# Rebuilding a mixer's decay weights without GpSimd, and scheduling small matmuls of one tiling as one operation

## The chip, the cores and the metric

One core of one Trainium2 chip. The metric is the device time in microseconds of one execution; lower is better. The kernel's engines are named as in the profile: PE (TensorE matmuls), PEld (TensorE weight loads), DVE (VectorE), ACT (ScalarE), POOL (GpSimd) and SP (SyncE, which issues the DMAs).

## What is computed

The network has two blocks over 512 tokens of width 1024 and a context of 256 tokens, all in fp32. The first block has two layers. Layer 0 mixes tokens with a gated delta rule (8 heads of width 128, both directions, called GDN here), layer 1 with a state space model (32 heads of width 64 in 8 groups of 4, both directions, called SSD here). Each layer ends in a mixture of 16 experts (MoE). A second block follows, which the change doesn't touch.

For the change two pieces of it matter. In SSD each head's output inside its stretch of 128 tokens is a weighted sum whose weights are

```python
acs = jnp.cumsum(dt_i * A, axis=1)
seg = jnp.where(tril, acs[:, :, None] - acs[:, None, :], -jnp.inf)
wts = jnp.einsum('btgn,bsgn->btsg', c_i, b_i)[..., None] * jnp.exp(seg) * dt_i[:, None]
```

The kernel makes the weights of both directions in one 128 x 512 tile W per head (four stretches of 128 x 128): exp of the smaller of the two directions' differences, times a factor Dm (dt of the forward direction on one side of the diagonal, dt of the backward one on the other), times the product of C and B, which the four heads of a group share. In GDN a triangular system of each stretch of 128 tokens is inverted: blocks of 32 by elimination, then blocks of 64 and 128 by products of blocks. Besides, six vectors per layer modulate the activations (the "ada" product, a 1024 x 6144 matrix for each layer times two vectors).

## The kernel before, in words

Every instruction is recorded first (`Rec.add`, line 126) with what it reads and writes, and a planner orders a whole stage at once (`Rec.flush`, line 217, and `Rec.schedule`, line 280). `Rec.cost` (line 164) gives each operation a duration, `LATENCY` (line 210) a delay between engines, and the planner takes, again and again, the operation that can start first, with a rank for ties that comes from the order in the program and the length of the chain behind it. Its result is one fixed order per engine; at run time each engine works through its own list in order. A stage may try several ranks and keep the best by its own count: GDN one, SSD three. An operation of PE writing to a PSUM tile is ordered behind earlier ones on the same 32 partitions of that tile. All instructions are issued from one line, 277, so the profile tells groups apart by tile names alone.

The stages, each one `flush`: the first norm and the first ada round (0 to 42 us), GDN (to about 800), the MoE's routing and gathering (to 850) and experts (to 1490), SSD's groups (to about 2080), SSD's output product, the second MoE, and block 2 from about 2760.

**The ada product** (`Mod.round`, line 937). One round is 8 k-steps; each k-step has four matmuls whose stationary operand is 32 columns wide (`self.sc`), each 128 x 512 and each writing another 32 partitions of one PSUM tile, so that they sit in four different column strips of the array. Each of the four is an operation of its own for the planner, and waits for its own 256 KB of weights. Round 0 is planned by itself, four rounds lie in GDN (as side work of heads 0, 6 and 7), one in the gathering of the first MoE. An fp32 matmul appears as two records in the trace.

**GDN** (`gdn`, line 550). Per head: four projections (tile px), each a product of split operands (a weight w is split into wh, its rounding, on ACT, and wl, the rest, on DVE or POOL, and three matmuls take the place of one); the squared norms of q and k (tile ssq, lines 689 to 695: two matmuls of 32 columns for q, then two for k); matrices L, GE and `at`; the elimination of 32 x 32 blocks on POOL (tiles x and D, 30 steps of two instructions); the inverse's products; and a scan of six steps. The inverse's products (lines 790 to 816) are, for blocks of 32 and then of 64, pB = L times U, and pU = T times B; for 64 the transpose pT comes first, as `pe.transpose` where d = 0 and as a matmul with the identity where d = 1. The loops run over the diagonal position (`cut`, 4 or 2 values, each a part of the array of its own) outside and over the six stretches of tokens inside. All outputs of one product lie in one PSUM tile.

**SSD** (`ssd`, line 1417). A preamble makes dt and the running sums cs, and writes their rows to DRAM. Then 8 groups of 4 heads; per head (lines 1495 to 1511):

```python
nc.sync.dma_start(x.rearrange("p t i -> p (t i)"), dbc(rscr[32 * d + h], 128))
g_.tensor_tensor(x, x, cs[:, :, 32 * d + h:32 * d + h + 1].to_broadcast([128, 4, 128]), op=OP.subtract)
...
v.tensor_tensor(W, R[0], R[1], op=OP.min)
s.activation(W, W, AF.Exp)
...
g_.tensor_tensor(Dm, K.m_le[:, None, :].to_broadcast([128, 4, 128]), dt[:, 0:4, h:h + 1].to_broadcast([128, 4, 128]), op=OP.mult)
...
v.tensor_tensor(W, W, Dm, op=OP.mult)
```

that is, per head, three POOL instructions of 128 x 512 (two on R, one on Dm), on DVE one minimum, four 128 x 128 pieces of Dm and one product, and one exp on ACT. After it come the group's four projections of x, B and C (px, pcx) and two of z (pz), whose low parts wl are made on DVE, for C and z on POOL; transposes (ptr), states (st), the product cb of C and B, its copy cbs on ACT, one DVE product of each W with cbs (line 1591), the heads' outputs py (16 matmuls of 64 columns in two PSUM tiles), the part from the states (pi, er), and the sums y and ssq, some of them on POOL. W has 4 buffers, R 4, Dm 1, cbs 2. The ring for weights holds 18 pieces.

Of the kernel before, what the change touches and what calls it, by code (L numbers as in the profile page):

```python
# [11 lines left out]
F32 = mybir.dt.float32  # L12
# [40 lines left out]
class Rec:  # L53
# [71 lines left out]

    def add(self, engine, method, a, k):
        reads, writes = [], []
# [8 lines left out]
        i = len(self.ops)  # L136
# [16 lines left out]
        if engine == "tensor":  # L153
            r = ww[0]
            key = r[0] + "#pe"
            q = (key, r[1] // 32 * 32, -(-r[2] // 32) * 32, 0, 1)
            lst = self.access.setdefault(key, [])
            preds.update(j for j, _, z in lst if q[1] < z[2] and z[1] < q[2])
# [3 lines left out]
        self.ops.append(dict(e=engine, m=method, a=a, k=k, preds=preds, names=names, cost=self.cost(engine, method, reads, writes, a, k), psum=any(self.tiles.get(r[0], (0, 0, 0))[2] for r in rr + ww)))  # L162
# [54 lines left out]
    def flush(self, trials=((0.0, 30.0),)):  # L217
# [166 lines left out]
KT = 8  # L384
# [165 lines left out]
def gdn(K, H, apply, w, ba_w, conv_w, a_log, dt_b, norm_g, scr, bscr, tscr, rscr, side, xc, w_out, gate, route):  # L550
# [111 lines left out]
    for h in range(NH):  # L662
# [27 lines left out]
        for j, a in enumerate((q, k_)):  # L690
            sq = per.tile([128, TT], F32, name="sq", tag="th", bufs=2)
            s.activation(sq, a, AF.Square, scale=0.5)
            for f in range(2):
                c = 32 * (2 * j + f)
                pe.matmul(pq[c:c + 32, :], K.ones[:, 0:32], sq[:, f * 384:(f + 1) * 384], start=True, stop=True)
# [94 lines left out]
        for m in (32, 64):  # L790
# [15 lines left out]
            for d, ra, ca in cut:  # L806
                for t in range(6):
                    pe.matmul(p[ra, t, :], L[ca, t, ra], Ud[ca, 1 - d, t, :] if m == 32 else U[ca, d, t, ca], start=True, stop=True, skip_group_check=True)
# [3 lines left out]
            for d, ra, ca in cut:  # L812
                for t in range(6):
                    pe.matmul(p[ra, t, :], Tr[d][ra, t, :], B[ra, t, :], start=True, stop=True, skip_group_check=True)
# [112 lines left out]
class Mod:  # L927
# [9 lines left out]
    def round(self, r):  # L937
# [479 lines left out]
def ssd(K, H, apply, w, wz, w_dt, conv_w, conv_b, a_log, dt_b, d_skip, norm_g, w_out, gate, keep, scr, rscr, side, route):  # L1417
# [46 lines left out]
    K.softplus(dt, a, tmp, sh, "W", 4)  # L1464
# [8 lines left out]
    for dst, ms in ((cs, (mid[:, 0, :], mid[:, 1, :])), (ea, (K.m_le, K.m_ge)), (we, (K.m_gt, K.m_lt)), (et, (K.ones, K.ones))):  # L1473
# [5 lines left out]
        s.activation(dst, p, AF.Copy if dst is cs else AF.Exp)  # L1479
    for j, x in enumerate((cs, ea)):  # L1480
# [4 lines left out]
        s.activation(rows, p.rearrange("p t i -> p (t i)"), AF.Copy)  # L1485
# [5 lines left out]
    for g in range(8):  # L1491
# [96 lines left out]
        cbs = grp.tile([128, 4, 128], F32, name="cbs", bufs=2)  # L1588
        s.activation(cbs, pcb, AF.Copy)
        for W in Ws:  # L1590
            v.tensor_tensor(W, W, cbs, op=OP.mult)
        py = [K.ps([128, 512], "py") for _ in range(2)]
        for i in range(2):
            for t in range(4):
                for r in range(2):
                    h = 2 * i + r
                    pe.matmul(py[i][64 * r:64 * r + 64, t * 128:(t + 1) * 128], xt[:, t, h * 64:(h + 1) * 64], Ws[h][:, t, :], start=(t == 0), stop=(t == 3))
# [887 lines left out]
```

## Time and profile before

| | us |
|---|---|
| median of 3 runs | 3717.8 (3711.24 to 3721.67) |
| the profiled execution | 3719.51 |
| its span, first to last instruction | 3717.7 |
| PE busy | 3442.1 (93%) |
| DVE busy | 1914.3 (51%) |
| ACT busy | 1105.9 (30%) |
| POOL busy | 662.7 (18%) |

The profile is one execution. "Busy" is the time in which at least one instruction of the engine runs; PE's records overlap, and their ends are modelled. The view by stretches gives, for each stretch of time, the busy time and instruction count of each engine, the granted TensorE clock (1.00 is 2.4 GHz, the lower level is 1.2) and the DMA engines' share. A view of one tile gives the shortest, median and longest duration of each kind of instruction on it.

### The profile page before, as it was taken

Reading aid. Unit: us, or ns where it says so; the run is one execution under the profiler, and the core shown is the slowest. Engines: PE = TensorE matmul, PEld = TensorE weight load, DVE = VectorE, ACT = ScalarE, POOL = GpSimd, SP = SyncE. Lnnn points to the kernel's source line nnn. Section 1 sums busy time; section 2 is a strip of 40 time slices with the busy share of each in tenths; the row PEclk is TensorE's granted clock in tenths of the full one; section 3 lists DMA queues with packets and bytes.
Section 4 is the critical chain, followed back from the end, with each engine's and each line's share of the span. In section 5 each row is a group of like instructions: output and inputs, shape, how many; then the busy total and the mean of one; then the engine's idle time right before and its main releaser. Section 6 shows DMA issues by size and latency. Waiting matters only on the chain. (4 is left out here: it accounts for less than half of the span.)

```text
span 3717.7 us, 55087 instructions
## 1 busy us (share of the span) xinstructions
PE 3442.1 (93%) x21457; PEld 2310.9 (62%) x21457; DVE 1914.3 (51%) x4006; ACT 1105.9 (30%) x2270; POOL 662.7 (18%) x849
## 2 busy tenths in 40 slices
PE   7999998899999999889999779988879999999999
PEld 4777775656444454667777664332247657878887
DVE  4657754453223222798888551371254574445552
ACT  3355443423111111433333322020032343333331
POOL 0546544301000000154444011020001000000000
PEclk9989999899999999999999889999999999999999
DMA  5422137354888887343333349899972302333332
GB/s 193 151 54 66 54 85 244 123 187 162 348 313 322 333 321 298 115 119 102 115 106 101 129 181 365 357 369 410 420 214 77 120 1 91 94 105 85 97 87 87
DMA packets 251649, 669.18 MB, mean 180 GB/s; under 512 B 72156, under 2 KB 85612, under 8 KB 202236
## 3 DMA queue, kind: packets, MB, share of 16 engines
q1 hardware_dynamic: 251388, 665.66, 50.7%
q8 instruction: 169, 2.77, 0.3%
q14 instruction: 92, 0.75, 0.1%
HBM read 644.26 MB, written 21.30 MB: 179 GB/s over the span
## 5 line engine op out<-in xcount | busy, mean ns | idle before, releaser
L277 DVE TENSOR_TENSOR wl<-w,wh 128x512 fp32r<-128x512 f32 (+3 forms) x452 | 320.9, 713 | 443.2 <-PE fu L277 67.6
L277 ACT ACTIVATE wh<-w 128x512 fp32r<-128x512 f32 (+3 forms) x500 | 307.0, 621 | 620.8 <-PE fu L277 120.6
L277 PE MATMUL eg<-we,xs 128*32 128x512 f32 (+1 forms) x1536 | 374.2, 597 | 9.5 <-DMA we<-moe_w 8.3
L277 PE MATMUL eu<-we,xs 128*32 128x512 f32 (+1 forms) x1536 | 324.4, 595 | 7.6 <-DMA we<-moe_w 7.6
L277 PE MATMUL ey<-we,hTs 128*32 128x512 f32 (+1 forms) x1536 | 295.9, 599 | 12.0 <-ACT hTs L277 9.0
L277 PE MATMUL px<-H,wl 128*128 128x512 f32 (+1 forms) x768 | 271.3, 372 | 6.4 <-DVE wl L277 6.4
L277 PE MATMUL px<-H,wh 128*128 128x512 f32 (+1 forms) x768 | 272.9, 376 | 2.8 <-ACT wh L277 1.6
L277 PE MATMUL px<-H1l,wh 128*128 128x512 f32 (+1 forms) x768 | 272.8, 369 | 0.0
L277 PE MATMUL ec<-we,xs 128*32 128x512 f32 x1024 | 237.5, 594 | 0.0
L277 DVE TENSOR_TENSOR yl<-ey,yh 64x512 fp32r<-64x512 f32 x64 | 44.1, 689 | 330.7 <-ACT yh L277 330.1
L277 POOL TENSOR_TENSOR wl<-w,wh 128x512 fp32r<-128x512 f32 x48 | 64.4, 1345 | 738.0 <-DVE H1l L277 651.5
L277 PEld LDWEIGHTS eg<-we,xs 128*32 128x32 f32 (+1 forms) x1536 | 98.7, 119 | 139.8 <-issue 94.6
L277 DVE SCALAR_TENSOR_TENSOR eth<-eth,eg 128x512 f32<-128x512 f32 x32 | 22.0, 688 | 312.9 <-ACT eth L277 312.9
L277 PEld LDWEIGHTS eu<-we,xs 128*32 128x32 f32 (+1 forms) x1536 | 94.8, 119 | 139.7 <-issue 97.2
L277 PEld LDWEIGHTS ey<-we,hTs 128*32 128x32 f32 (+1 forms) x1536 | 98.6, 120 | 120.9 <-issue 60.9
L277 PEld LDWEIGHTS px<-H,wh 128*128 128x128 f32 x768 | 146.3, 194 | 30.3 <-issue 6.4
L277 PEld LDWEIGHTS px<-H,wl 128*128 128x128 f32 x768 | 145.2, 194 | 28.9 <-DVE wl L277 8.5
L277 PEld LDWEIGHTS px<-H1l,wh 128*128 128x128 f32 x768 | 145.2, 194 | 23.3 <-issue 4.6
L277 ACT ACTIVATE eth<-eg 128x512 f32<-128x512 f32 x32 | 19.1, 596 | 463.2 <-PE eg L277 434.4
L277 PE MATMUL eyc<-we,hcTs 128*32 128x256 f32 x1024 | 143.4, 379 | 0.0
L277 POOL TENSOR_TENSOR x<-D 48x30 f32<-48x30 f32 (+14 forms) x240 | 127.1, 530 | 90.8 <-DVE D L277 73.9
L277 POOL TENSOR_TENSOR D<-D,x 48x30 f32<-48x30 f32 (+14 forms) x240 | 133.6, 557 | 17.9
(1041 smaller groups left out, 7816.1 us busy)
## 6 DMA issues: line engine op xcount, KB each, us to landing
we<-moe_w SPq DMA_DIRECT2D x384, 1024.0 KB, 7.2
w<-ada_w SPq DMA_DIRECT2D x192, 256.0 KB, 4.9
w<-w_gu SPq DMA_DIRECT2D x88, 256.0 KB, 3.0
w<-gdn_w SPq DMA_DIRECT2D x64, 256.0 KB, 3.2
w<-ssd_w SPq DMA_DIRECT2D x64, 256.0 KB, 4.0
R<-ssd_rows SPq DMA_DIRECT2D x64, 256.0 KB, 4.7
w<-w_mix SPq DMA_DIRECT2D x48, 256.0 KB, 2.7
w<-w_dn SPq DMA_DIRECT2D x40, 256.0 KB, 2.6
```

What stands on the lines that cost most here:

```text
L277: getattr(getattr(self.nc, o["e"]), o["m"])(*o["a"], **o["k"])
```

## The change

`Rec.together()` is a new context: the PE operations recorded inside it become one operation of the planner, with their dependencies united and their costs added, and are issued back to back. It is put around: the four ada matmuls of a k-step; the four squared-norm matmuls of a GDN head (both squares are now made first, in two tiles); pT, pB and pU of the inverse, each, with the loops turned round (six stretches outside, diagonal positions inside); and each PSUM tile of py (8 matmuls). In pT the transposes become matmuls with the identity for both values of d.

SSD's decays leave POOL. The rows of the forward direction are loaded into W itself (6 buffers), those of the backward one into R (3 buffers). Per stretch of 128 tokens ACT adds the column of -cs to W (`Identity` with a bias), and DVE takes, in one instruction, R plus its column and the minimum. After exp, W is not touched until cb is there. From cb DVE makes two masked copies per group, cb0 and cb1, straight from PSUM; per head and stretch ACT scales cb0 by dt and DVE adds cb1 times the other dt (tile Dm, in R's buffers); one product of W with Dm ends it.

```diff
+    @contextmanager
+    def together(self):
+        assert self.run is None
+        self.run = []
+        yield
+        self.run = None
...
+        if i < len(self.ops):
+            o = self.ops[i]
+            o["preds"] |= preds
+            o["names"] |= names
+            o["cost"] += cost
+            o["more"].append((method, a, k))
+            return
...
-            getattr(getattr(self.nc, o["e"]), o["m"])(*o["a"], **o["k"])
+            for m, a, k in [(o["m"], o["a"], o["k"])] + o.get("more", []):
+                getattr(getattr(self.nc, o["e"]), m)(*a, **k)
...
+        sqs = []
+        for a in (q, k_):
+            sqs.append(per.tile([128, TT], F32, name="sq", tag="th", bufs=2))
+            s.activation(sqs[-1], a, AF.Square, scale=0.5)
+        with nc.together():
+            for c in range(4):
+                j, f = divmod(c, 2)
+                pe.matmul(pq[32 * c:32 * c + 32, :], K.ones[:, 0:32], sqs[j][:, f * 384:(f + 1) * 384], start=True, stop=True)
...
-                for d, ra, ca in cut:
+                with nc.together():
                     for t in range(6):
-                        if d:
+                        for d, ra, ca in cut:
                             pe.matmul(p[ra, t, :], U[ra, d, t, ra], K.ident[ra, ra], start=True, stop=True, skip_group_check=True)
-                        else:
-                            pe.transpose(p[ra, t, :], U[ra, d, t, ra], K.ident[ra, ra])
...
-            for d, ra, ca in cut:
+            with nc.together():
                 for t in range(6):
-                    pe.matmul(p[ra, t, :], Tr[d][ra, t, :], B[ra, t, :], start=True, stop=True, skip_group_check=True)
+                    for d, ra, ca in cut:
+                        pe.matmul(p[ra, t, :], Tr[d][ra, t, :], B[ra, t, :], start=True, stop=True, skip_group_check=True)
...
-            for c in range(4):
-                nc.tensor.matmul(p[32 * c:32 * c + 32, :], self.sc[:, k, :], wt[:, c, :], start=(k == 0), stop=(k == KT - 1))
+            with nc.together():
+                for c in range(4):
+                    nc.tensor.matmul(p[32 * c:32 * c + 32, :], self.sc[:, k, :], wt[:, c, :], start=(k == 0), stop=(k == KT - 1))
...
-                x = tmp.tile([128, 4, 128], F32, name="R", bufs=4)
+                x = tmp.tile([128, 4, 128], F32, name="WR"[d], bufs=6 - 3 * d)
                 nc.sync.dma_start(x.rearrange("p t i -> p (t i)"), dbc(rscr[32 * d + h], 128))
-                g_.tensor_tensor(x, x, cs[:, :, 32 * d + h:32 * d + h + 1].to_broadcast([128, 4, 128]), op=OP.subtract)
                 R.append(x)
-            W = tmp.tile([128, 4, 128], F32, name="W", bufs=4)
-            v.tensor_tensor(W, R[0], R[1], op=OP.min)
+            W = R[0]
+            for t in range(4):
+                s.activation(W[:, t, :], W[:, t, :], AF.Identity, bias=cs[:, t, h:h + 1])
+                v.scalar_tensor_tensor(W[:, t, :], R[1][:, t, :], cs[:, t, 32 + h:33 + h], W[:, t, :], op0=OP.add, op1=OP.min)
             s.activation(W, W, AF.Exp)
-            Dm = tmp.tile([128, 4, 128], F32, name="Dm", bufs=1)
-            g_.tensor_tensor(Dm, K.m_le[:, None, :].to_broadcast([128, 4, 128]), dt[:, 0:4, h:h + 1].to_broadcast([128, 4, 128]), op=OP.mult)
-            for t in range(4):
-                v.scalar_tensor_tensor(Dm[:, t, :], K.m_ge, dt[:, t, 32 + h:33 + h], Dm[:, t, :], op0=OP.mult, op1=OP.add)
-            v.tensor_tensor(W, W, Dm, op=OP.mult)
             Ws.append(W)
...
-        cbs = grp.tile([128, 4, 128], F32, name="cbs", bufs=2)
-        s.activation(cbs, pcb, AF.Copy)
-        for W in Ws:
-            v.tensor_tensor(W, W, cbs, op=OP.mult)
+        cbs = [grp.tile([128, 4, 128], F32, name=f"cb{d}", bufs=1) for d in range(2)]
+        for cb_, m in zip(cbs, (K.m_le, K.m_ge)):
+            v.tensor_tensor(cb_, pcb, m[:, None, :].to_broadcast([128, 4, 128]), op=OP.mult)
+        for r, W in enumerate(Ws):
+            h = 4 * g + r
+            Dm = tmp.tile([128, 4, 128], F32, name="Dm", tag="R", bufs=3)
+            for t in range(4):
+                s.activation(Dm[:, t, :], cbs[0][:, t, :], AF.Copy, scale=dt[:, t, h:h + 1])
+                v.scalar_tensor_tensor(Dm[:, t, :], cbs[1][:, t, :], dt[:, t, 32 + h:33 + h], Dm[:, t, :], op0=OP.mult, op1=OP.add)
+            v.tensor_tensor(W, W, Dm, op=OP.mult)
```

## Rows read from the trace of the kernel before

**Rows 1.** Stretches: length, busy PE, PEld, DVE, ACT, POOL (count); clock, DMA share, GB/s

```profile
78.00:581.00 503.00, 470.94 (x3449) 374.42 (x3448) 320.41 (x870) 231.70 (x544) 256.14 (x426) 0.94 0.32 92
...
760.00:850.00 90.00, 79.14 (x504) 49.57 (x503) 54.40 (x118) 20.04 (x50) 4.33 (x6) 0.92 0.48 173
...
1581.00:2046.00 465.00, 427.86 (x2290) 352.06 (x2289) 409.34 (x610) 157.21 (x278) 227.06 (x178) 0.95 0.36 108
2046.00:2080.00 34.00, 20.15 (x125) 15.28 (x123) 25.42 (x45) 10.67 (x20) 7.49 (x7) 0.80 0.18 60
```

**Rows 2.** PE's waits, 1581 to 2046: us in total, times, longest

```profile
PE pz L277 <- POOL wl L277: 19.2, 5, 4.5
PE st L277 <- DVE xw L277: 6.8, 8, 1.7
```

**Rows 3.** DVE's groups by line and shape, 1581 to 2046

```profile
L277 DVE SCALAR_TENSOR_TENSOR Dm<-cst,dt,Dm 128x128 f32<-128x128 f32 x124 | 100.0, 861 | 2.6 <-POOL Dm L277 2.6
L277 DVE TENSOR_TENSOR W<-R 128x512 f32<-128x512 f32 x32 | 34.8, 1102 | 0.0
L277 DVE TENSOR_TENSOR W<-W,Dm 128x512 f32<-128x512 f32 x32 | 30.4, 949 | 0.9
L277 DVE TENSOR_TENSOR W<-W,cbs 128x512 f32<-128x512 f32 x28 | 21.3, 759 | 1.3 <-ACT cbs L277 1.3
```

**Rows 4.** Tiles Dm and R: shortest/median/longest ns, first and last start

```profile
L277 DVE SCALAR_TENSOR_TENSOR Dm<-cst,dt,Dm x128: 334/1130/1451, 1578.7 to 2032.6; 128x128 f32<-128x128 f32 x128
...
L277 DVE TENSOR_TENSOR W<-R x32: 672/1030/1789, 1589.7 to 2023.1; 128x512 f32<-128x512 f32 x32
```

**Rows 5.** POOL's groups, 1581 to 2046

```profile
L277 POOL TENSOR_TENSOR R<-R,cs 128x512 f32<-128x512 f32 x64 | 79.9, 1264 | 31.6 <-DMA R<-ssd_rows 15.1 <-ACT xt L277 8.5 <-DVE W L277 4.7
L277 POOL TENSOR_TENSOR wl<-w,wh 128x512 fp32r<-128x512 f32 x42 | 55.2, 1318 | 68.4 <-DMA w<-ssd_w 20.1 <-PE pz L277 19.0 <-DVE wl L277 9.7
...
L277 POOL TENSOR_TENSOR Dm<-cst,dt 128x512 f32<-128x512 f32 x31 | 34.9, 1126 | 28.9 <-DVE W L277 27.4 <-DMA ssd_scratch<-y 1.5
```

**Rows 6.** ACT's scaled 128x128 copy in GDN (tile vb)

```profile
L277 ACT ACTIVATE vb<-vT,cols x96: 386/399/407, 99.9 to 735.6; 128x128 f32<-128x128 f32 x96
```

**Rows 7.** ACT's longest wait in SSD's groups, and the DMA of R

```profile
ACT W L277 <- DVE W L277: 130.8, 27, 10.2
...
R<-ssd_rows SPq DMA_DIRECT2D x64, 256.0 KB, 4.7
```

**Rows 8.** PE in order of time: one ada matmul alone, then four together

```profile
126.02 1.05 PE L277 MATMUL ada<-w,sc 128*32 128x512 f32 x2
...
112.65 1.06 PE L277 MATMUL ada<-w,sc 128*32 128x512 f32 x8
```

**Rows 9.** Tile ada alone, by stretches: length, busy PE, PEld, ACT; clock, DMA

```profile
78.00:552.00 474.00, 18.50 (x64) 2.75 (x64) 0.60 (x1) 0.94 0.29 82
552.00:760.00 208.00, 49.83 (x192) 8.63 (x192) 1.79 (x3) 0.95 0.57 177
760.00:850.00 90.00, 20.53 (x64) 3.26 (x64) 0.60 (x1) 0.92 0.48 173
```

**Rows 10.** Tile ssq alone, one stretch: length, busy PE, PEld, DVE, ACT, POOL

```profile
78.00:552.00 474.00, 13.23 (x56) 2.19 (x56) 0.00 (x0) 3.43 (x7) 0.00 (x0) 0.94 0.29 82
```

**Rows 11.** PE in order of time: pU of two heads, the start of pB for 64

```profile
205.48 0.86 PE L277 MATMUL pU<-B,Td 32*32 32x32 f32 x48
...
353.14 1.21 PE L277 MATMUL pU<-B,Td 32*32 32x32 f32 x48 [0.60 <-ACT B L277]
...
355.41 0.39 PE L277 MATMUL pB<-U,L 64*64 64x64 f32 x5
...
357.59 0.39 PE L277 MATMUL px<-H1l,wh 128*128 128x256 f32 x1
358.72 1.31 PE L277 MATMUL pU<-B,Tr 64*64 64x64 f32 x24
```

**Rows 12.** POOL in order of time: the elimination of GDN's head 6 starts

```profile
581.38 0.24 POOL L277 TENSOR_TENSOR x<-D 48x30 f32<-48x30 f32 x1 [18.14 <-DVE D L277]
```

More of the change, by code (lines that the diff above doesn't have):

```diff
@@ L3 @@
 import math
-from contextlib import ExitStack
+from contextlib import ExitStack, contextmanager
 import numpy as np
@@ L124, in region, with record @@
         return name, p0, last // row + 1, 0, row * size
-    def add(self, engine, method, a, k):
+    @contextmanager
[3 more added lines that the diff above has]
+        yield
+        self.run = None
+    def add(self, engine, method, a, k):
+        if self.run is None or engine != "tensor":
+            return self.record(len(self.ops), engine, method, a, k)
+        if not self.run:
+            self.run.append(len(self.ops))
+            self.record(self.run[0], engine, method, a, k)
+            self.ops[-1]["more"] = []
+        else:
+            self.record(self.run[0], engine, method, a, k)
+    def record(self, i, engine, method, a, k):
         reads, writes = [], []
@@ L157, in add @@
             lst = self.access.setdefault(key, [])
-            preds.update(j for j, _, z in lst if q[1] < z[2] and z[1] < q[2])
+            preds.update(j for j, _, z in lst if j != i and q[1] < z[2] and z[1] < q[2])
             lst[:] = [t for t in lst if not (q[1] <= t[2][1] and t[2][2] <= q[2])]
@@ L161, in add @@
         names = {r[0] for r in rr + ww}
-        self.ops.append(dict(e=engine, m=method, a=a, k=k, preds=preds, names=names, cost=self.cost(engine, method, reads, writes, a, k), psum=any(self.tiles.get(r[0], (0, 0, 0))[2] for r in rr + ww)))
+        cost = self.cost(engine, method, reads, writes, a, k)
+        if i < len(self.ops):
[5 more added lines that the diff above has]
+            return
+        self.ops.append(dict(e=engine, m=method, a=a, k=k, preds=preds, names=names, cost=cost, psum=any(self.tiles.get(r[0], (0, 0, 0))[2] for r in rr + ww)))
     def cost(self, engine, method, reads, writes, a, k):
@@ L689, in gdn @@
         pq = K.ps([128, 384], "ssq")
[L690 to L695, printed above, removed]
+        sqs = []
[6 more added lines that the diff above has]
+                pe.matmul(pq[32 * c:32 * c + 32, :], K.ones[:, 0:32], sqs[j][:, f * 384:(f + 1) * 384], start=True, stop=True)
         sq = K.nm.tile([128, 512], F32, name="ssq_", tag="nm", bufs=3)
@@ L805, in gdn @@
             p = K.ps([128, 6, m], "pB")
-            for d, ra, ca in cut:
+            with nc.together():
                 for t in range(6):
-                    pe.matmul(p[ra, t, :], L[ca, t, ra], Ud[ca, 1 - d, t, :] if m == 32 else U[ca, d, t, ca], start=True, stop=True, skip_group_check=True)
+                    for d, ra, ca in cut:
+                        pe.matmul(p[ra, t, :], L[ca, t, ra], Ud[ca, 1 - d, t, :] if m == 32 else U[ca, d, t, ca], start=True, stop=True, skip_group_check=True)
             B = tmp.tile([128, 6, m], F32, name=f"B{m}")
@@ L943, in round @@
             wt = K.wtile(self.w[r, k], [128, 4, 512])
-            for c in range(4):
-                nc.tensor.matmul(p[32 * c:32 * c + 32, :], self.sc[:, k, :], wt[:, c, :], start=(k == 0), stop=(k == KT - 1))
+            with nc.together():
+                for c in range(4):
+                    nc.tensor.matmul(p[32 * c:32 * c + 32, :], self.sc[:, k, :], wt[:, c, :], start=(k == 0), stop=(k == KT - 1))
         row = K.nm.tile([128, 512], F32, name="adarow", tag="nm", bufs=3)
@@ L1463, in ssd @@
     v.tensor_tensor(a, p, al[:, 1:2, :].to_broadcast(sh), op=OP.add)
-    K.softplus(dt, a, tmp, sh, "W", 4)
+    K.softplus(dt, a, tmp, sh, "W", 6)
     v.scalar_tensor_tensor(a, dt, -1.0, al[:, 0:1, :].to_broadcast(sh), op0=OP.mult, op1=OP.mult)
@@ L1478, in ssd @@
             pe.matmul(p[:, :, c], ms[d], a[:, 0:n, c], start=True, stop=True)
-        s.activation(dst, p, AF.Copy if dst is cs else AF.Exp)
+        if dst is cs:
+            s.activation(dst, p, AF.Copy, scale=-1.0)
+        else:
+            s.activation(dst, p, AF.Exp)
     for j, x in enumerate((cs, ea)):
@@ L1484, in ssd @@
         rows = K.nm.tile([64, 512], F32, name="rows", tag="nm", bufs=3)
-        s.activation(rows, p.rearrange("p t i -> p (t i)"), AF.Copy)
+        s.activation(rows, p.rearrange("p t i -> p (t i)"), AF.Copy, scale=1.0 if j else -1.0)
         nc.sync.dma_start(rscr[64 * j:64 * j + 64], rows)
@@ L1587, in ssd @@
             pe.matmul(pcb[:, t, :], BT[:, t * 128:(t + 1) * 128], CT[:, t * 128:(t + 1) * 128], start=True, stop=True)
-        cbs = grp.tile([128, 4, 128], F32, name="cbs", bufs=2)
-        s.activation(cbs, pcb, AF.Copy)
-        for W in Ws:
-            v.tensor_tensor(W, W, cbs, op=OP.mult)
+        cbs = [grp.tile([128, 4, 128], F32, name=f"cb{d}", bufs=1) for d in range(2)]
[8 more added lines that the diff above has]
+            v.tensor_tensor(W, W, Dm, op=OP.mult)
         py = [K.ps([128, 512], "py") for _ in range(2)]
         for i in range(2):
[L1594 to L1597, printed above, removed]
+            with nc.together():
+                for t in range(4):
+                    for r in range(2):
+                        h = 2 * i + r
+                        pe.matmul(py[i][64 * r:64 * r + 64, t * 128:(t + 1) * 128], xt[:, t, h * 64:(h + 1) * 64], Ws[h][:, t, :], start=(t == 0), stop=(t == 3))
         for i in range(2):
```

3 lines of the change are left out of this document (1 added, 2 removed).

## The prediction

> **What bounds the kernel now.** I read the page first: PE is busy 93% of the span, so a time can only fall where PE waits or where its own work shrinks. Then the view by stretches for the three stages that the change touches [rows 1]. In GDN (78 to 581 us) PE is busy 470.9 of 503 us: PE is the bound, and its own work counts. In SSD's groups (1581 to 2046) PE is busy 427.9 of 465 us, but DVE is busy 409.3, 88%, and the granted clock is 0.95: two engines run close to their limit, and PE loses 37 us to waits and some 5% of 428, 21 us, to the lower clock, together 58. The list of PE's waits says whom it waits for: the low parts of z's weights, which POOL makes, 19.2 us, and DVE's xw, 6.8 us [rows 2]; the rest is small change of other DVE work.
>
> Next, why DVE is so full. The groups of DVE instructions show four that belong to the decays: 100.0, 34.8, 30.4 and 21.3 us, 186.5 in all, in 465 [rows 3]. The view of one tile shows that their durations are not their own: the 128x128 piece of Dm takes 334 ns at best and 1130 in the median, the minimum of 128x512 takes 672 at best and 1030 in the median [rows 4]. At the best durations the four groups would take 124 x 0.334 + 92 x 0.672 = 103 us, so 83 us are stretching. In the same time POOL runs instructions of 1.1 to 1.3 us on the same kind of tiles, 227 us of them [rows 1, 5]; the median piece of Dm lasts about as long as one of those. I read this as DVE being held up while POOL works.
>
> **Part 1, SSD.** Removed from POOL: R, 79.9 us, and Dm, 34.9 us, of its 227 [rows 1, 5]; left are the low parts wl (55.2) and the sums. Removed from DVE: the 186.5 us above. Added to DVE, per head: four pieces for the minimum, four for Dm (0.334 each) and one product (0.672), 3.34 us; per group two masked copies, taken at 0.672. For the 31 heads and some 7.5 groups of this stretch: 31 x 3.34 + 15 x 0.67 = 114 us if nothing holds DVE up. Half of POOL's work stays (112 of 227), so up to half of the 83 us of stretching may stay as well. DVE falls by 186.5 - 114 = 72 us at most and by 72 - 42 = 30 at least, to 337 to 379 of 465.
>
> Added to ACT: eight 128x128 pieces per head. The nearest row, a scaled copy of that size, takes 0.399 us [rows 6]; 31 x 8 x 0.4 = 99 us, so ACT goes from 157 to some 256 of 465 (55%), less 4 for the copies cbs. By throughput that is hidden. The additions with a bias wait for R's rows and W's rows, 4.7 us after their issue [rows 7], as POOL did (15.1 us of its idle time [rows 5]); queued behind them on ACT are the rounded weights wh, for which PE waits. I cost this at nothing, since W has six buffers where four are in use, so the first heads of a group can load before the group before is done; if that cover is gone, it costs the rival below. ACT already stands 130.8 us waiting for DVE's minimum, once for 10.2 us [rows 7], without a wait of PE worth a row, which is what the cover looks like. The same 64 loads stay on SP's queue, only into other buffers.
>
> What PE gets back lies between 0 and the 58 us it loses. DVE's sure relief is 30 us and the largest wait of PE is POOL's, which loses half its work; I take 30.
>
> At the end of the stage the order of the work costs something: after the last cb DVE had four products of 0.67, 2.7 us; now it has two masked copies and four heads of 4 x 0.334 + 0.67, 9.4 us. In that stretch DVE is busy 25.4 of 34 us [rows 1], so little of it finds room: +5 (0 to +7). For the other groups the next group's projections cover it. Putting py's 8 matmuls together saves a switch of tiling or two per group; I leave it at nothing. SSD: -25 (-58 to +7).
>
> **Part 2, ada.** A single ada matmul holds PE for 1.05 us, and four together hold it for 1.06 [rows 8]: they run side by side in four strips, so whoever issues them apart pays again for each. The planner counts a quarter for each, and scatters them. There are 8 k-steps per round, each worth about 1.0 us as a group. In GDN's first round 64 records (32 matmuls) take 18.5 us [rows 9]: 8 groups take 8, -10. Of the next three rounds (49.8 us for 24 k-steps) only what runs before 581 counts, since from there to the end of GDN the chain runs through POOL's elimination for heads 6 and 7, which starts then [rows 12], and PE has room beside it; about a quarter of 49.8 - 24 = 26, which is 6, of which I take 4: -4. In MoE's gathering 20.5 us become 8 [rows 9], -12, of which I take half, because PE has 11 us of waits there already [rows 1], for weights among others: -6 (-12 to 0).
>
> **Part 3, ssq.** By the same row the second pair of matmuls is free when both pairs run together: 13.2 us for 7 heads [rows 10] halve, -7. The price is that q's square waits in its buffer for k's; the two share a ring of two with the tanh tiles, which then waits one square longer on ACT, off PE's path.
>
> **Part 4, the inverse.** Nearly all heads run pU for 32 in 1.21 us, one place runs the same 48 records in 0.86 [rows 11]. The planner's ties there went by the length of the chain, that is with the diagonal positions turning fastest, as the new loops do for all; this is inferred from the code, the trace doesn't show the order. I take 0.86 for pU and pB of 32. For 64 pB and pT together run from 355.41 to 357.59, 2.18 us, and pU takes 1.31 [rows 11]; as groups of 24 records with two positions side by side I take 0.9 each, 1.8 and 0.9. Turning transposes into matmuls adds 6 records, counted in. Per head 0.35 + 0.35 + 0.4 + 0.4 = 1.5 us, for five heads before 581: -8 (-12, if every one runs at the lower clock, to 0).
>
> The rows speak for running side by side: 0.86 is less than 1.21. The Trainium skill speaks against it: TensorEngine Tiling (Array Packing), section Restrictions and Gotchas, says that different row tiles cannot access the same PSUM bank simultaneously, and here all positions write to one tile. By that rule part 4 would be 0 and the sum 6 us higher; the 0.86 us is evidence against the rule in this place.
>
> **GDN's sum:** -10 - 4 - 7 - 8 = -29 us of PE's work. PE is busy 94% there, and work that goes partly uncovers waits that it hid; I take three quarters, -22 (-38 to 0; the planner makes a wholly new order, and that alone may move some us either way).
>
> **Sum:** -25 - 22 - 6 = -53 us. The profiled execution took 3719.5 (span 3717.7, 1.8 around it), so 3666.5; the median of the runs is 1.7 lower: **3665 us**. Block 2, the second MoE and SSD's output are not touched.
>
> **Rivals.**
> - *DVE stays SSD's pace.* The remaining POOL work still holds DVE up, and the handing to and fro between ACT and DVE in small pieces eats the relief. For it: half of POOL's time stays [rows 5]. Against: DVE is relieved of at least 30 us by count. SSD then gives only its longer end, +5: -22 - 6 + 5 = -23, 3695 us.
> - *GDN's new order gives nothing.* One order is planned, without a second try. Then -25 - 6, 3687 us.
> - *The row tiles' rule holds.* Part 4 gives nothing: 3671 us. By that rule; the 0.86 us of rows 11 speaks against.
> - *Everything is released.* PE in SSD gets all 58 back, GDN all 38, MoE 12: -103, 3615 us. Against: DVE would still be at 73%.
> - *Slower: ACT's queue.* ACT takes its list in order. Between cb and py it now alternates with DVE through four heads (8 us of DVE work), and at a group's start it waits for rows (4.7 us [rows 7]). If wh of the next projections is queued behind both, PE stands for up to 12.7 us per group, 8 x 12.7 = 102: with -22 - 6 that is 3791 us. It decides from 28 / 8 = 3.5 us per group with no other gain in SSD, 7 with the 30. For it: wh shares ACT's queue. Against: the planner knows these waits, and 130.8 us of waits on the same queue do no harm now [rows 7].
>
> **How the numbers follow.** The forecast has 0.50, DVE's pace 0.18, GDN's order 0.10, the rule 0.04, everything released 0.10, ACT's queue 0.08. About 0.3%, 11 us, is what a measurement of this kernel can tell from no change, so faster means below 3706.6. The forecast's own range is 3640 to 3690. The range for all takes in DVE's pace with some of its loss, 3708, and reaches down to where everything is released, 3615; outside remain ACT's queue and the far ends of the others. Faster: all but ACT's queue and a half of DVE's pace, whose own spread reaches past 3706: 0.83. Same 0.09, slower 0.08.
>
> **What would show it.** Right: the pieces of Dm with a median near 0.35 us; DVE in SSD's groups below 380 per 465; POOL near 110; the wait of pz for POOL's wl under 8 us; SSD's groups 20 to 35 us shorter; tile ada near 1.0 us per eight records; ssq halved; pU for 32 near 0.86 us in every head. Wrong: Dm's median still near 1 us (DVE's pace), PE waiting for ACT's wh by tens of us (the slower rival), GDN ending no earlier, or pU still at 1.2 us with the new loops (the rule).

## The result, and the profile after

The changed kernel takes 3660.3 us in the median of 4 runs (3659.8 to 3663.8), beside 3719.7 (3711.2 to 3723.4) for the kernel before on the same chip: ratio 0.9834, 95% interval 0.9814 to 0.9855, so 1.7% faster, against 3665 forecast. The total came within 5 us, in part by luck: SSD gave 14 us more than forecast, GDN 6 us less, and the other stages together lost 3 us that nobody had forecast.

Where the two profiled executions part, read from the first or last instruction of a tile that marks a stage's end:

| stage, up to | before, us | after, us | change in the stage |
|---|---|---|---|
| end of GDN (last X with its part) | 790.1 | 773.9 | -16.2 |
| MoE's gathering (first eg) | 892.1 | 869.7 | -6.2 |
| its experts (X to its scratch) | 1501.7 | 1483.8 | +4.5 |
| SSD's preamble (first fm) | 1554.5 | 1538.7 | +2.1 |
| SSD's groups and norm (Rs) | 2099.6 | 2045.0 | -38.8 |
| the rest (last dn) | 3713.2 | 3654.9 | -3.7 |

Sum -58.3. The experts and what follows SSD run the same code in both kernels. A second profile of the changed program (the run after_again below) has the experts within 1 us of this and the rest 4 us longer, so the last row may be chance.

The page of the kernel after, busy times, and its clock in 40 slices:

```profile
PE 3359.7 (92%) x21505; PEld 2255.5 (62%) x21505; DVE 1848.2 (51%) x4086; ACT 1181.0 (32%) x2518; POOL 555.4 (15%) x753
PEclk9999989899999999999999889999999999999999
```

The view by stretches, after (columns as in [rows 1]): GDN up to head 6's elimination, SSD's groups, and all of SSD from its first fm to Rs:

```profile
78.00:572.60 494.60, 429.15 (x3510) 355.81 (x3509) 329.69 (x901) 236.22 (x562) 255.83 (x426) 0.94 0.29 82
1565.20:1991.40 426.20, 401.80 (x2282) 338.88 (x2281) 339.78 (x679) 231.00 (x514) 119.23 (x83) 0.98 0.38 118
1538.70:2045.00 506.30, 459.53 (x2603) 386.46 (x2602) 402.33 (x798) 263.93 (x579) 134.37 (x97) 0.96 0.39 123
```

and the last of these stretches in the kernel before:

```profile
1554.50:2099.60 545.10, 487.12 (x2603) 400.00 (x2602) 469.77 (x718) 188.12 (x330) 242.83 (x193) 0.93 0.37 114
```

SSD: the groups take 426 us where they took 465 [rows 1], 38.8 less. (Both stretches are cut at the same distances from the ends of the longer one, so the longer one loses the same by construction.) PE's idle time in the longer stretch fell by 11.2 (58.0 to 46.8) and its own work by 27.6, for the same 2603 records. GDN tells another story: PE does 42 us less work than in [rows 1], but the stretch is only 8 us shorter. PE now idles 65 us where it idled 32. The two stretches don't hold quite the same work (118 records of ada before, 88 after), so here is the whole stage, before and after:

```profile
42.00:790.10 748.10, 689.10 (x4914) 535.71 (x4916) 452.90 (x1228) 320.82 (x764) 328.43 (x559) 0.94 0.38 114
42.00:773.90 731.90, 638.85 (x4962) 505.99 (x4964) 455.19 (x1227) 320.34 (x764) 329.68 (x559) 0.94 0.38 116
```

PE's work falls by 50 us, its idle time rises by 34 (59.0 to 93.1), and 16 us remain.

PE's waits in SSD's groups, after:

```profile
PE px L304 <- DVE wl L304: 17.6, 9, 4.5
PE py L304 <- DVE W L304: 4.0, 7, 1.7
```

The wait for POOL's wl [rows 2] is gone; the largest is now for weights that DVE splits. DVE's groups in that stretch (us, mean ns; the idle time before them), after:

```profile
L304 DVE SCALAR_TENSOR_TENSOR Dm<-cb,dt,Dm 128x128 f32<-128x128 f32 x112 | 51.0, 490 | 2.9 <-ACT Dm L304 2.8
L304 DVE SCALAR_TENSOR_TENSOR W<-R,cs,W 128x128 f32<-128x128 f32 x128 | 47.7, 428 | 13.9 <-ACT W L304 8.4 <-DMA R<-ssd_rows 2.5 <-ACT bt L304 1.7
L304 DVE TENSOR_TENSOR xw<-xt,wend 128x256 f32<-128x256 f32 x70 | 30.5, 448 | 0.6 <-ACT xt L304 0.3 <-PE st L304 0.2
```

and the view of tiles Dm and W (shortest, median, longest ns), after:

```profile
L304 DVE SCALAR_TENSOR_TENSOR Dm<-cb,dt,Dm x128: 334/341/1382, 1583.3 to 2011.0; 128x128 f32<-128x128 f32 x128
L304 DVE SCALAR_TENSOR_TENSOR W<-R,cs,W x128: 333/340/1383, 1571.9 to 1965.2; 128x128 f32<-128x128 f32 x128
```

The median piece of Dm fell from 1130 ns [rows 4] to 341; the mean of 490 says that a part of the pieces is still held up.

PE in order of time in GDN, after (start, length): the products of 32, pU of 64, and an ada k-step:

```profile
246.67 0.61 PE L304 MATMUL pB<-Ud,L 32*32 32x32 f32 x48
249.16 0.62 PE L304 MATMUL pU<-B,Td 32*32 32x32 f32 x48 [0.69 <-ACT B L304]
253.64 0.92 PE L304 MATMUL pU<-B,Tr 64*64 64x64 f32 x24
91.99 1.07 PE L304 MATMUL ada<-w,sc 128*32 128x512 f32 x8
```

The 0.62 us of pU for 32 answers to the 1.21 of [rows 11], both at a granted clock of 1.00. The view by stretches for one tile alone (78 to 850; the second number is PE's busy time) prices every regrouped product; before, for pT, pB, pU, ssq and ada: 16.82, 27.44, 23.94, 15.73, 88.85. Here pU, before:

```profile
78.00:850.00 772.00, 23.94 (x576) 21.71 (x576) 18.08 (x48) 0.94 0.39 118
```

and after, where the five tiles have 9.21, 14.63, 14.81, 8.09, 73.75:

```profile
78.00:850.00 772.00, 14.81 (x576) 12.68 (x576) 18.05 (x48) 0.94 0.38 118
```

Summed, the inverse's three tiles go from 68.2 to 38.7 us. But pT's and pB's records run partly at the same time, and the sums count that time twice. With their records merged, PE is busy with the three tiles for 59.3 us before and 34.8 after: the inverse saves 24 us. Tile ada after, by the stretches of [rows 9]:

```profile
78.00:552.00 474.00, 9.58 (x64) 1.62 (x64) 0.58 (x1) 0.94 0.29 81
552.00:760.00 208.00, 44.31 (x192) 8.05 (x192) 1.76 (x3) 0.93 0.57 181
760.00:850.00 90.00, 19.87 (x64) 3.63 (x64) 0.60 (x1) 0.97 0.46 164
```

The first round halves; the later rounds stay near the 49.8 and 20.5 us of [rows 9]. What took back what PE saved stands in the groups of PE's instructions, after (78 to 760; behind the bar the idle time ahead of them):

```profile
L304 PE MATMUL pB<-U,L 64*64 64x64 f32 x192 | 9.2, 257 | 4.9 <-POOL D L304 2.7 <-ACT U L304 2.2
L304 PE MATMUL pB<-Ud,L 32*32 32x32 f32 x384 | 5.4, 204 | 25.9 <-DMA Ud<-gdn_inverses 13.0 <-DVE D L304 12.9
```

PE comes to pB before the blocks that POOL's elimination sends through DRAM are back: 25.9 us in place of 5.3 before. Two waits make up most of it. The view puts the second one down to D, which pB doesn't read; the two loads of pB's blocks Ud were issued at 480.9 and 481.4 us and took 3.5 us to land, so this wait ends with the blocks too. PE in order of time, after:

```profile
336.09 0.86 PE L304 MATMUL pB<-Ud,L 32*32 32x32 f32 x48 [9.87 <-DMA Ud<-gdn_inverses]
485.19 0.86 PE L304 MATMUL pB<-Ud,L 32*32 32x32 f32 x48 [12.85 <-DVE D L304]
```

### The profile page after: what moved, and what is told of

It is laid out like the page before. It is cut to its first block, busy times and chain, and to the rows that moved or that the text cites. A ratio compares the mean times of both kernels' runs of the same rounds, so it can differ in the third digit from the quotient of the medians.

```text
span 3659.1 us, 55424 instructions
## 1 busy us (share of the span) xinstructions
PE 3359.7 (92%) x21505; PEld 2255.5 (62%) x21505; DVE 1848.2 (51%) x4086; ACT 1181.0 (32%) x2518; POOL 555.4 (15%) x753
```

## The experiments

All are edits of the changed kernel, unless said otherwise. The runs come from several chips, so the ratio to the kernel before on the same chip is what is compared (95% interval).

| run | median, us | ratio | GDN ends | SSD, first fm to Rs |
|---|---|---|---|---|
| after | 3660.3 | 0.9834 (0.9814 to 0.9855) | 773.9 | 506.3 |
| e1_groups_only | 3707.7 | 0.9951 (0.9933 to 0.9969) | 773.4 | 547.0 |
| e2_decays_only | 3678.0 | 0.9875 (0.9856 to 0.9895) | 787.4 | 499.0 |
| e3_pool_ballast | 3719.7 | 0.9977 (0.9965 to 0.9989) | 776.4 | 556.2 |
| e4_diag_outside | 3696.0 | 0.9918 (0.9889 to 0.9947) | 797.7 | 514.2 |
| e5_sums_on_dve | 3664.3 | 0.9845 (0.9812 to 0.9878) | 778.4 | 499.9 |
| e6_no_pool | 3655.2 | 0.9813 (0.9784 to 0.9841) | 773.9 | 493.5 |
| e7_ada_ssq_apart | 3667.1 | 0.9848 (0.9818 to 0.9878) | 766.8 | 511.8 |
| e8_transpose_kept | 3687.7 | 0.9904 (0.9880 to 0.9928) | 800.1 | 506.0 |
| e9_gather_ada_no_pool | 3644.7 | 0.9775 (0.9753 to 0.9797) | 767.3 | 496.2 |
| e10_and_py_apart | 3664.9 | 0.9843 (0.9821 to 0.9864) | 764.6 | 519.7 |
| e11_ada_apart_in_gdn | 3708.0 | 0.9948 (0.9929 to 0.9968) | 819.0 | 507.1 |
| after_again | 3670.3 | 0.9850 (0.9828 to 0.9873) | 774.1 | 505.9 |

Where GDN's program is the same (after, e1, e3, e5, e6, after_again) it ends between 773.4 and 778.4; where SSD's is (after, e4, e7, e8, e11, after_again) it takes 505.9 to 514.2. Differences below some 6 us in the first of these columns, and some 9 in the second, say nothing.

**The two halves apart.** e1 keeps the grouping of ada, ssq and the inverse and takes SSD from the kernel before (py apart); e2 is the kernel before with SSD's decays changed and nothing grouped.

> Only the grouped matmuls (ada, squared norms, the inverse's pT, pB, pU with the loops turned); SSD's decays and py as before. My theory: the two halves of the change work in different stages and add up. The first MoE's start then comes as early as with the whole change (some 16 us at the end of GDN, 4 of them given back in the experts by waits for expert weights), SSD lasts as long as before: about 3702 us (3695 to 3708). Rival (the planner's order, which carries over from stage to stage, made SSD faster, not the decays): SSD shortens here too, and the time is below 3685.

> Only SSD's decays without GpSimd; every matmul ungrouped, transposes as transposes. My theory: SSD shortens by what the traces show, 39 us, and GDN not at all: about 3680 us (3673 to 3690), the median piece of Dm on DVE at 0.34 us. Rival (py's grouping or the new order of GDN carries SSD's gain): above 3695.

Both as expected: 0.49% and 1.25%, together 1.74 beside 1.66 for the whole. SSD's gain is the decays', GDN's that of the grouping. The grouping of py is in neither half, and the whole gains no more than the two halves do. The stretch of SSD in e2, with PE idle for 32.4 us:

```profile
1559.20:2058.20 499.00, 466.60 (x2603) 392.71 (x2602) 403.68 (x798) 265.44 (x578) 132.36 (x97) 0.98 0.41 125
```

**POOL put back.** e3 gives POOL twelve reads per group whose result nobody uses:

```diff
+        for j in range(12):
+            junk = tmp.tile([128, 4, 128], BF, name="junk", bufs=1)
+            g_.tensor_tensor(junk, bt[:, 0:4, :], cs[:, :, j:j + 1].to_broadcast([128, 4, 128]), op=OP.subtract)
```

> The whole change, with twelve more POOL instructions of 128x512 per group, each reading two SBUF operands and writing a tile that nobody reads: the POOL time that the change removed (some 115 us) is put back, DVE's and ACT's work is the new one. Theory (DVE is held up while POOL works on SBUF): the pieces of the minimum and of Dm on DVE go from a median of 0.34 us towards 1 us, or their mean from 0.43 and 0.49 to 0.7 or more, DVE in the groups rises by 30 us or more, and most of SSD's 39 us is lost: 3685 to 3700 us. Rival (the gain comes from fewer or better placed DVE instructions, POOL's own time is idle cover): medians stay at 0.34, time 3660 to 3666.

SSD went back to 556 us, beyond the kernel before: more than either theory said. DVE's groups in the ballast run (1536 to 2010):

```profile
L304 DVE SCALAR_TENSOR_TENSOR Dm<-cb,dt,Dm 128x128 f32<-128x128 f32 x112 | 62.6, 595 | 2.7 <-ACT Dm L304 2.7
L304 DVE TENSOR_TENSOR xw<-xt,wend 128x256 f32<-128x256 f32 x70 | 55.9, 821 | 6.5 <-ACT xt L304 6.5
L304 DVE SCALAR_TENSOR_TENSOR fm<-px,cw,fm 128x511 f32<-128x511 f32 x58 | 43.0, 741 | 12.8 <-ACT fm L304 12.5
```

PE's waits in the same stretch:

```profile
PE st L304 <- DVE xw L304: 25.1, 36, 2.2
PE py L304 <- DVE W L304: 11.3, 7, 3.8
PE pz L304 <- POOL wl L304: 0.2, 1, 0.2
```

PE hardly waits for POOL itself, so the loss does not come through POOL's own list. No instruction of DVE was added, and yet xw rose from 448 to 821 ns, while fm<-px, which has one of its inputs in PSUM, stays at the 741 it has after. The medians of Dm and W stayed at 340 ns and their means rose to 595 and 507, less than I had expected (medians towards 1000, or means of 700 and more); the largest rise was xw's. That POOL at work holds DVE up is shown. The Trainium skill says which instructions: SBUF — State Buffer, section Who interferes with whom, has a DVE instruction with two SBUF inputs contend with a GpSimd instruction that reads SBUF, and one with at most one SBUF input (outside the 2-port modes) not. The 821 and the unmoved 741 agree with it.

**POOL taken away.** e5 moves the sums er, y and ssq from POOL to DVE, e6 also the low parts wl.

```diff
-            g_.tensor_tensor(u[0], u[0], u[1], op=OP.add)
+            v.tensor_tensor(u[0], u[0], u[1], op=OP.add)
...
-            g_.tensor_tensor(y, y, u[0], op=OP.add)
+            v.tensor_tensor(y, y, u[0], op=OP.add)
...
-            wt = K.wpair(wz[2 * g + i], [128, KT, 128], low=g_)
+            wt = K.wpair(wz[2 * g + i], [128, KT, 128])
```

> The whole change, and in SSD's groups POOL's three sums (er, y and ssq, 64 us of its 119 in the 426 us of the groups) made by DVE. Theory (POOL at work is what stretches DVE): the 41 sums cost DVE 41 x 0.68 = 28 us, and about half of the 30 to 40 us by which Dm, W, xw and wl still lie above their medians comes back: DVE stays at 335 to 355 per 426, the mean of Dm falls from 490 towards 410. PE waits only 24 us there, so the time hardly changes: 3655 to 3668. Rival (DVE's count of instructions is what matters, POOL's time does not): DVE rises by the full 28 us to 367, the means stay, PE waits 10 to 20 us more for DVE: 3670 to 3680.

> As the run before, and the low parts wl of C's and z's weights made by DVE too: POOL does nothing in SSD's groups. Theory: every 128x128 piece of Dm and of the minimum takes 334 to 345 ns, mean as well as median; xw falls below 350 ns in the mean; DVE has 64 us more of work and 35 to 45 us less of stretching, 355 to 370 per 426; PE's clock and waits near those of the whole change: 3655 to 3675. Rival (the stretching has another source, such as ACT or the DMAs): the means stay above 400 and DVE is busy over 95%, SSD's groups 20 us longer or more: 3680 or above.

DVE's groups in e6 (1540 to 2000), where POOL does nothing:

```profile
L304 DVE SCALAR_TENSOR_TENSOR W<-R,cs,W 128x128 f32<-128x128 f32 x128 | 37.4, 343 | 8.1 <-ACT wh L304 3.4 <-ACT W L304 3.1 <-DMA R<-ssd_rows 1.6
L304 DVE SCALAR_TENSOR_TENSOR Dm<-cb,dt,Dm 128x128 f32<-128x128 f32 x124 | 36.8, 344 | 2.6 <-ACT Dm L304 2.5
```

Now mean and median agree (343 ns), as the theory said: the rest of the stretching was POOL's. In e5 DVE did 41 sums more and was busy 366.7 of 460 us (1540 to 2000), beside 369.4 after. Per 426 us, as I had put it, that is 340 (335 to 355 expected). The mean of its Dm pieces fell to 343 ns (towards 410 was expected): what held Dm up were the sums alone, which run while it is made. e6 has 389.7 of 460, which is 361 per 426 (355 to 370 expected). Its xw stayed at 418 (not below 350), so those 418 ns are not POOL's doing. SSD takes 493.5, 13 less than after. In total neither is clear of the changed kernel: e5's ratio lies within its interval, e6's just below it, and the intervals overlap.

**The loops' order.** e4 turns pT, pB and pU back to diagonal positions outside, stretches inside, still in one group. The planned order of every engine stays as in the changed kernel, but for the records inside a group.

```diff
-                    for t in range(6):
-                        for d, ra, ca in cut:
+                    for d, ra, ca in cut:
+                        for t in range(6):
```

> The whole change with the inverse's loops as before the change: diagonal positions outside, stretches inside, still grouped, transposes still as matmuls. Theory (neighbouring matmuls on different parts of the array run side by side although they write one PSUM tile): pU for 32 takes 1.15 to 1.2 us again instead of 0.62, pU for 64 1.25 instead of 0.92, some 2 us per head, and the time rises by 3 to 12 us, to 3663 to 3672. Rival (row tiles writing to one PSUM bank take turns, the gain comes from grouping alone): both stay at their new values and the time at 3660.

PE in order of time, diagonal outside:

```profile
250.67 1.37 PE L304 MATMUL pB<-Ud,L 32*32 32x32 f32 x48
253.06 1.40 PE L304 MATMUL pU<-B,Td 32*32 32x32 f32 x48
259.36 1.43 PE L304 MATMUL pU<-B,Tr 64*64 64x64 f32 x24
```

The same 48 records take 1.40 us in place of 0.62, both with the granted clock at 1.00 around them. The three products, merged as above, take 69.7 us in place of 34.8, and GDN ends 23.8 us later, where I had expected 3 to 12 in all. Positions in turn do run side by side into one PSUM tile: the row tiles' rule, which the forecast had set against the 0.86 of [rows 11], does not hold for this pattern. (The rule is the Trainium skill's, TensorEngine Tiling (Array Packing), section Restrictions and Gotchas; the 0.62 us decide against it.)

**The transposes.** e8 keeps the transposes where d = 0, inside the group, so that transposes and matmuls alternate.

```diff
-                            pe.matmul(p[ra, t, :], U[ra, d, t, ra], K.ident[ra, ra], start=True, stop=True, skip_group_check=True)
+                            if d:
+                                pe.matmul(p[ra, t, :], U[ra, d, t, ra], K.ident[ra, ra], start=True, stop=True, skip_group_check=True)
+                            else:
+                                pe.transpose(p[ra, t, :], U[ra, d, t, ra], K.ident[ra, ra])
```

> The whole change, but in pT the transposes of the first diagonal block stay transposes, inside the group. Theory (the turn into matmuls only adds records and costs or saves next to nothing): pT and pB of 64 together take 1.3 to 1.6 us, time within 4 us of the whole change: 3656 to 3665. Rival (a transpose between matmuls breaks the running side by side, or its mode costs a drain of the array each time): pT alone grows by 0.5 us or more per head, 4 us or more in all, and GDN ends 5 to 10 us later: 3665 to 3672.

Tile pT alone, transposes alternating (after: 9.21):

```profile
78.00:850.00 772.00, 24.91 (x144) 16.12 (x144) 3.93 (x8) 0.92 0.39 119
```

The rival holds, and far beyond its number: 2 us per head, and GDN ends 26 us later. In the kernel before, the six transposes of a head run in one block: the starts of its 18 records show just two wide gaps in seven of the eight heads. There pT took 16.8, and in e4, as matmuls one position after the other, 15.5. So transposes in a block cost little, and alternating them with matmuls costs 15.7 over the changed kernel's 9.2. At a granted clock of 1.00 the records of e8's pT start 0.11 to 0.17 us apart (from 263.55), where most of those before start 0.06 apart (from 355.59). What it is in the alternation that takes the time these runs don't show.

**Which grouping pays in GDN.** e7 has ada and ssq apart, as before, with the inverse grouped. e11 has ada apart in GDN alone. e9 has that too, and ssq apart, on top of e6. e10 is e9 with py apart.

```diff
-            with nc.together():
+            with nc.together() if (self.name, r) in (("0", 0), ("1", 2)) else nullcontext():
                 for c in range(4):
                     nc.tensor.matmul(p[32 * c:32 * c + 32, :], self.sc[:, k, :], wt[:, c, :], start=(k == 0), stop=(k == KT - 1))
```

> The whole change with ada's and ssq's matmuls as operations of their own, as before; the inverse stays grouped, SSD as changed. Which part gave GDN its 16 us? If ada and ssq gave most (my sum: 21 of 29 us of PE's work, and all of the 6 in the gathering), GDN ends 10 to 13 us later than with the whole change and the gathering takes its 6 us again, of which the experts give back half: 3672 to 3682. Rival (the inverse gave most, since the run with its loops outside lost 24 us): GDN ends within 5 us of the whole change: 3662 to 3670.

> The whole change, with ada apart in GDN alone (ssq and the gathering's round stay grouped). Theory (as for the run that joins the parts): PE is busy over 455 of 494 us from 78 to 572, its granted clock there 0.96 to 0.99, GDN ends by 765 to 770 all the same or sooner, the gathering at 94 to 98: 3650 to 3658. Rival (ssq's grouping, not ada's, cost those 7 us): GDN ends at 772 to 778 with ada apart: 3658 to 3664.

> Put together from the parts that paid: SSD without POOL, ada grouped in the first stage and in the MoE's gathering alone, ssq apart, the inverse grouped. Theory (in GDN the single ada matmuls only fill what the elimination on POOL leaves idle, so grouping them there frees nothing): GDN ends at 765 to 770 as with ada and ssq apart, the gathering takes 94 to 98, SSD from its first fm to Rs 490 to 496; against the whole change on the same chip -7 in GDN and -8 to -12 in SSD, so 3640 to 3650 if the whole change stands at 3660 there. Rival (the 7 us of GDN were the spread of one execution, and the experts take back what comes before them): GDN ends at 772 to 778, and only SSD's share is left: 3648 to 3656.

> As the run before, with py's matmuls as operations of their own too. Theory (grouping py holds the eight matmuls back until all the heads' weights W are there, and saves no switch that counts; the run with the decays alone had SSD 7 us shorter with py apart): SSD from its first fm to Rs 484 to 492, the total 2 to 8 us below the run before. Rival (together they save switches between tilings): SSD 3 us longer or more than in the run before.

> The whole change, unaltered, on the same chip as the three runs beside it, so that they can be compared with it: 3655 to 3667; GDN ends at 773 to 779, SSD from its first fm to Rs takes 500 to 512. Its own spread from run to run is what a difference to the others has to exceed.

e7 met neither theory: with 26 us of ada's and 6.5 of ssq's work back on PE, GDN ended earlier, at 766.8. Only the gathering lost, 105.1 us in place of 95.8. Its whole GDN stage:

```profile
42.00:766.80 724.80, 665.76 (x4960) 503.85 (x4962) 446.55 (x1224) 321.15 (x763) 326.20 (x559) 0.96 0.39 117
```

That is 23 us less work of PE than in the kernel before, the same 59.0 us of idle time, and a stage 23 us shorter. e11, which I expected to be faster, is the slowest of the group. e9 and e11 differ inside GDN's stage by ssq's grouping alone, and its ends lie 52 us apart. PE's waits, 78 to 760, in e11:

```profile
PE pB L304 <- DMA Ud<-gdn_inverses: 40.7, 6, 14.7
```

and in e9:

```profile
PE pB L304 <- DMA Ud<-gdn_inverses: 1.9, 5, 0.7
```

All five profiles with ssq apart (the kernel before, e2, e7, e9, e10) have at most 7.0 us of waits at this pB for its blocks; the nine with ssq grouped have 25 to 41, with those that the view puts down to D. So one group of eight records per head turns the planned order of the whole stage into one in which PE reaches the inverse ahead of the elimination. Why, I did not follow up: the edit binds the four matmuls together, and it also has both squares made first, which fill the ring of two that they share with the tanh tiles. No run groups ada in GDN with ssq apart, so what ada's grouping alone is worth there is open.

The clock in a stretch with one of these waits, after:

```profile
280.00:380.00 100.00, 80.81 (x620) 67.56 (x619) 67.25 (x173) 42.01 (x105) 67.94 (x117) 0.91 0.21 57
```

and e9:

```profile
280.00:380.00 100.00, 93.16 (x697) 76.39 (x697) 71.58 (x198) 50.03 (x129) 72.69 (x125) 0.98 0.24 62
```

With PE busy for 81 of the 100 us the granted clock is 0.91, with 93 it is 0.98. No ada matmul lies in this stretch in either run. In e9 the wait of 9.9 us for pB is gone, and PE makes more of the scan's products here (tile p, 180 records in place of 108); these runs don't separate the two.

py alone in SSD's stretch, grouped (e9):

```profile
1529.20:2025.40 496.20, 19.03 (x256) 14.47 (x256) 11.90 (x16) 0.97 0.40 125
```

and apart (e10; before 35.97, after 23.23):

```profile
1527.20:2046.90 519.70, 35.91 (x256) 28.15 (x256) 11.91 (x16) 0.96 0.39 118
```

17 us of PE's work, and SSD 23.5 us longer: the rival to my theory. Against the whole change on the same chip (after_again, 3670.3, above the 3655 to 3667 expected) e9, at 3644.7, is 25.6 us faster, with ratios to before whose intervals don't meet: it beats both kernels, as expected. By the profiles, whose spans lie 18.7 apart, SSD without POOL gives 9.7 and GDN 6.8.

## Why the prediction was right, and where its steps were not

**What bounded SSD: right.** DVE was held up by POOL. The signs came: medians near 0.34 us, DVE 339.8 of 426 (371 per 465, in the range of 337 to 379), ACT 231 of 426 (252 per 465; 256 forecast), pz's wait gone; POOL 119 us in the shorter stretch, near 112. ACT's queue, the slower rival, did not come: no wait of PE for wh is worth a row. DVE's pace came only in part: PE's largest waits are now for DVE, and to take the rest of POOL's work away brings 13 us net (e6). How much of the 39 us came through DVE, and how much through POOL's own list (the 19.2 us of pz [rows 2]), no run separates.

**SSD's size: too small, and which term was it?** Forecast were -25 us, measured -38.8. The "+5" for a longer end failed: from the last cb to Rs took 49.6 us before and 47.7 after. For the rest, two readings disagree. By the profile of the whole change, the 30 us that I took back of PE's 58 were about right: waits gave 11.2, and of PE's own 27.6 us py gave 12.7 (36.0 to 23.2), which leaves 14.9, the granted clock having gone from 0.93 to 0.96; 26 in all. Then the step that failed is "Putting py's 8 matmuls together saves a switch of tiling or two per group; I leave it at nothing", where the runs show 12.7 to 17 us of PE. But e2, with py apart, has SSD at 499.0 us, 46 below the kernel before: by that run the decays alone gave more than the 30, and py's grouping nothing on top (after has 506.3, with PE idle for 14 us more than in e2). Without POOL's work the grouping did pay, 23.5 us (e9, e10). So which of the two terms was too small is open.

**GDN: the wrong parts counted.** The forecast booked 21 us for grouping ada and ssq and 8 for the inverse, and took three quarters. The runs show the reverse. With the inverse alone grouped (e7), PE's 23 us less of work shorten the stage by 23: there "PE is the bound, and its own work counts" holds in full. With ada and ssq grouped too, PE works 27 us less still, idles 34 us more, and the stage ends 7 us later. So the step that failed is that this work counts as well: with ssq grouped PE reaches pB ahead of the elimination and waits there, 25.9 us. The inverse's order and its transposes gave GDN its gain (e4, e8).

Two prices were off beside that. For ada, "8 k-steps per round, each worth about 1.0 us as a group" holds in the first round (18.5 to 9.6). The next three go from 49.8 to 44.3 us where the step says 24, since each matmul of a group still waits for its own weights; only 4 us of that were booked, so the sum hardly felt it. ssq halves, as said. For the inverse, the "0.86 for pU and pB of 32" came from a place at the lower clock: positions in turn take 0.86 us at a granted clock of 0.50 and 0.62 at 1.00. The clock at the place of [rows 11] before, and the same group at that clock after:

```profile
205.00:207.00 2.00, 1.97 (x53) 1.51 (x52) 0.00 (x0) 0.97 (x4) 1.61 (x6) 0.50 0.00 0
339.35 0.86 PE L304 MATMUL pU<-B,Td 32*32 32x32 f32 x48 [2.40 <-ACT B L304]
339.30:340.30 1.00, 0.86 (x48) 0.73 (x48) 0.97 (x2) 0.02 (x1) 0.58 (x1) 0.50 0.00 0
```

Over all heads the forecast's prices after (4.4 us per head) fit the 34.8 us for eight. Those before were too low: the rows add up to 5.9 per head, and the eight heads took 59.3 us, 7.4 each. In five of them a part or all of the inverse ran at 0.50 before, and pU for 32 took 1.21 in four of the eight, not in "nearly all heads" (0.86, 1.58, 1.88 and 1.89 in the others). And eight heads gained, not five: 24 us in place of 8.

**Gathering: size right (6.2), reason not.** The ada records still take 19.9 us there (8 were forecast), since each waits for its piece of weights: from 801.5 to 804.2 us five of them start 0.7 us apart, each as its piece lands. e7 shows that the grouping brings the gain: over the stage PE is busy 86.8 us with it (clock 0.96), 93.5 without (0.90), and 90.2 before (0.92). How the one brings the other is open.

**The row tiles' rule: refuted here** by e4; the 4% were fair for it. "That alone may move some us either way" was far too small for a new order: ssq's grouping moves GDN by 52.

**A slip in a sum.** In the rival "Everything is released" 58, 38 and 12 add up to 108; the 103 holds only with the +5 for the longer end. The forecast doesn't use it; the lower end of the range would be 3610.

## What to carry to other kernels

Small matmuls in different parts of the array pay only when they follow each other in turn: 1.40 us became 0.62 by swapping two loops, and transposes between the matmuls of pT undid it there. When an engine's instructions have a median far above their shortest, look at which engine works on the same memory at that time, and count its work as their cost. When a stage is near its bound, price the chain that is late next before booking an engine's saved work, and undo each part alone: here the groupings of ada and ssq took back part of what the inverse's gave, and leaving them out of GDN, with POOL's rest gone, gave 0.7% more. And look up the granted clock of a row before taking its time as a price.

## What I had not expected of the hardware

Alternating transposes with matmuls in pT takes 24.9 us for 144 records, more than the transposes in one block (16.8, the same 144) and matmuls in their place (9.2, with 192). POOL's work in SBUF cost DVE's instructions with two inputs in SBUF up to twice their time in the mean (xw 418 ns without POOL, 448 with its sums and wl, 821 with the ballast), and those with an input in PSUM nothing (fm<-px 741 in all three). And after the two long waits PE ran at the lower clock: the two pB that had waited 9.87 and 12.85 us take 0.86 us at a granted clock of 0.50, where the one at 246.67, without such a wait, takes 0.61 at 1.00. Ahead of them PE had been busy for 1.2 us of 11 and for 0.3 of 13.1, and the clock had fallen in the wait, at 328.4 and 475.1 us.
